# Two 256-column gating projections joined to one of 512 columns, and the spatial product moved behind the next projection's first steps

## The chip, the cores and the metric

The kernel runs on one core of a Trainium2 chip. The metric is the device time of one execution in microseconds; the time of a kernel is the median of its runs. Five engines work beside each other and wait for each other through semaphores: TensorE (PE) multiplies, VectorE (DVE) and ScalarE (ACT) work on tiles, GpSimd (POOL) does small pieces, and SyncE (SP) issues nearly all transfers. A matmul writes to PSUM, which has eight banks of 512 float32 columns; DVE or ACT must read a bank out before another result can take it.

## What is computed

One layer of a hybrid trunk for 1024 positions of 1024 channels. The part that matters here, cut from the reference:

```python
n = rms_norm(x, mix_norm_g[l])
proj = jnp.einsum('bsd,de->bse', n, w_in[l])
q, k, v, bg, cg, xh, su, sv = jnp.split(proj, cuts, axis=-1)
y_a = chunked_rel_attention(...)           # 8 heads of 64
y_b = gated_short_conv(bg, cg, xh, conv_w[l])
y_c = spatial_gating(su, sv, sg_ln_g[l], sg_ln_b[l], sg_w[l], sg_b[l])
...
# spatial_gating(u, v, ...), 256 channels each, blocks of 128 positions
u = jax.nn.gelu(u, approximate=False)
v = layer_norm(jax.nn.gelu(v, approximate=False), ln_g, ln_b)
mixed = jnp.einsum('gts,bnsgc->bntgc', tril(sg_w), vb) + sg_b
return u * mixed
```

Group norms, an output projection, a squared-ReLU MLP and a final norm follow; the change does not touch them.

## The kernel before

Every float32 product is made of three matmuls of a rounded high part and a remainder (`mm3`, lines 64 to 66): high by high, high by low, low by high. An operand is split by one ACT copy and one DVE subtraction (`split`, lines 52 and 53).

The front of the program runs in this order: the norm of x and the value projection; the key and query projections of head pair 0 (`qk_projs(0)`); `sgu`, the spatial gating; then the attention loop over 64 steps (four pairs, two heads, eight query tiles). Inside the loop the remaining projections run as fillers, in steps of three matmuls, and a table of knots (`target`) says how many filler steps are due at each attention step. The instructions of each engine are put in order by a scheduler that goes by program order and its own costs; each engine then works its list strictly in order.

In `sgu` the weights of the projection of v (`ws`, 256 columns) are split into slots that the attention uses later (`pth`, `ptl`). For each of eight tiles of 128 positions `token_proj` runs 24 matmuls of 256 columns into a PSUM tile `sv`; ACT applies GELU (`gv`, line 608), DVE and POOL do the layer norm (lines 610 to 616, `bs`, `mv`, `ms`, `rs`), and ACT and DVE split the result into `vh` and `vl`. Then a second loop does the same projection for u (`wu`, tile `su`, 24 matmuls of 256 columns for each tile, GELU at line 624). After it come the load of ACT's exponential table (line 625), `between()` (the expansion of the heads' operands, with the copies `v` at lines 300 and 301), and the spatial product: four groups `sg` of three matmuls of 512 columns, each read out by two DVE instructions (line 635, `u<-sg,cols,u`).

PSUM tiles are named by tags. `acc_tile` takes the tags of the list `ring` in turn. During `sgu` the list is `["acc", "S", "PT", "acc", "S"]`; after it, it is `["acc"]`, and a tag has two buffers. `s` are the scores of a step, `pr` its exponentials (line 485), `pt` their transposes, `pth` and `ptl` the split of these, `av` the product with the values. `kc` is both the raw weights of a key projection and, later, its result; `wh_k`, `wl_k`, `wh_q` and `wl_q` are split weights of pair 1 and take the slots (two for each tag) in which `wu` stood before.

Of the kernel before, what the change touches and what calls it, by code (L numbers as in the profile page):

```python
# [15 lines left out]
P = 128  # L16
# [4 lines left out]
HD = 64  # L21
# [9 lines left out]
def trunk(ctx, tc, x, mix_g, w_in, rb_rev, conv_w, sg_ln_g, sg_ln_b, sg_w, sg_b,  # L31
# [13 lines left out]
    def big(tag, shape, dt, name):  # L45
        return L.tile(shape, dt, tag=tag, bufs=SLOTS[tag], name=name)
# [16 lines left out]
    def mm3(ps, sh, sl, mh, ml, start, stop, **kw):  # L63
        PE.matmul(ps, lhsT=sh, rhs=mh, start=start, stop=False, **kw)  # L64
        PE.matmul(ps, lhsT=sh, rhs=ml, start=False, stop=False, **kw)  # L65
        PE.matmul(ps, lhsT=sl, rhs=mh, start=False, stop=stop, **kw)  # L66
# [69 lines left out]
    def acc_tile(name, tag=None):  # L136
        if tag is None:
            ring["i"] += 1
            tag = ring["tags"][ring["i"] % len(ring["tags"])]
        return psA.tile([P, 1024 if tag == "S" else HALF], F32, tag=tag, bufs=2,  # L140
                        name=name)[:, :HALF]
# [33 lines left out]
    def load_moving(c0, m, name, place):  # L175
        w = Moving(c0, m, name, place)
        for j in range(NK // w.kk):
            w.load(j)
            run(w.split(j))
        return w.ws  # L180

    def place_w(name):
        return lambda j, kk, m: (W.tile([P, kk, m], F32R, tag="wh", name=f"{name}h{j}"),
                                 W.tile([P, kk, m], F32R, tag="wl", name=f"{name}l{j}"))
# [6 lines left out]
    def token_proj(t, ws, m, name, between=None):  # L191
        hf, sl = t // 4, slice((t % 4) * P, (t % 4 + 1) * P)
        ps = acc_tile(name)[:, :m]
        for k in range(NK):
            if between and k == 4:
                between()
            mm3(ps, n.hi(hf, k)[:, sl], n.lo(hf, k)[:, sl], ws[k][0], ws[k][1],
                k == 0, k == NK - 1)
        return ps
# [247 lines left out]
    def scores(i):  # L447
        p, j, t, kb0, nfar = where(i)
        q2, kh, kl = heads[p, j]
        if t == 0:  # L450
            biases[p, j] = bias_tile(2 * p + j)
        if j == 0 and t == 0:
            ya[p] = big("VY", [P, T], F32, f"ya{p}")
        if j == 0 and t % 4 == 0:
            lsum[p, t // 4] = sm.tile([P, 8], F32, tag="lsum", bufs=4, name=f"lsum{p}{t // 4}")
        qs = q2[:, t * P:(t + 1) * P]
        s = prs[i] = wide(f"s{p}{j}{t}")

        near = slice((t - 1) * P, (t + 1) * P) if t > 3 else slice(0, max(2, t + 1) * P)
        end = HALF + near.stop - near.start  # L460
        if t > 3:
            ks = slice(kb0 * P, (t - 1) * P)
            PE.matmul(s[:, P:HALF], lhsT=qs, rhs=kh[:, ks], start=True, stop=False)
            PE.matmul(s[:, P:HALF], lhsT=qs, rhs=kl[:, ks], start=False, stop=True)
            V.memset(s[HD:P, P:P + HD], NEG)
        PE.matmul(s[:, HALF:end], lhsT=qs, rhs=kh[:, near], start=True, stop=False)
        PE.matmul(s[:, HALF:end], lhsT=qs, rhs=kl[:, near], start=False, stop=True)

    def softmax(i):
        p, j, t, kb0, nfar = where(i)  # L470
        s, bias = prs[i], biases[p, j]
        a = P if t > 3 else HALF
        b = a + (t - kb0 + 1) * P
        w = min(2, t + 1) * P
        st = sm.tile([P, 4], F32, tag="st", name=f"st{i}")
        V.tensor_tensor_reduce(out=s[:, b - w:b], in0=s[:, b - w:b], in1=bias[:, 256 - w:256],
                               op0=ALU.add, op1=ALU.max, scale=1.0, scalar=NEG, accum_out=st[:, 0:1])
        if nfar:
            V.tensor_reduce(st[:, 1:2], s[:, a:b - w], axis=AX.X, op=ALU.max)
            V.tensor_scalar(st[:, 2:3], st[:, 0:1], st[:, 1:2], -1.0, op0=ALU.max, op1=ALU.mult)  # L480
        else:
            V.tensor_scalar(st[:, 2:3], st[:, 0:1], -1.0, None, op0=ALU.mult)
        pr = AP_.tile([P, 640], F32, tag="P", bufs=3, name=f"pr{i}")
        lc = 2 * (t % 4) + j
        A.activation(pr[:, :b - a], s[:, a:b], AF.Exp, bias=st[:, 2:3],  # L485
                     accum_out=lsum[p, t // 4][:, lc:lc + 1])
        prs[i] = pr
# [95 lines left out]
    def sgu(u, between):  # L583
        sgw = raw_tile([P, 4, P], "sgw")
        load(sgw, sg_w.rearrange("g t s -> t g s"))
        ps = acc_tile("sgwT")
        for g in range(4):
            PE.transpose(ps[:, g * P:(g + 1) * P], sgw[:, g, :], ident)
        wsT = tmp("wsT").rearrange("p (g t) -> p g t", g=4)
        A.activation(wsT, ps.rearrange("p (g t) -> p g t", g=4), AF.Copy)  # L590
        G.affine_select(out=wsT, in_=wsT, pattern=[[0, 4], [1, P]], compare_op=ALU.is_ge,
                        fill=0.0, base=0, channel_multiplier=-1)
        wsh, wsl = [AP_.tile([P, 4, P], F32R, tag="P", bufs=3, name=f"wsT{a}") for a in "hl"]
        split(wsT, wsh, wsl)
        lnr = raw_tile([P, 2, 256], "lnr")
        load(lnr[:, 0, :], sg_ln_g.partition_broadcast(P))
        load(lnr[:, 1, :], sg_ln_b.partition_broadcast(P))
        ln = AP_.tile([P, 2, 256], F32, tag="P", bufs=3, name="ln")
        V.tensor_copy(ln, lnr)

        ws = load_moving(C_SU + 256, 256, "ws", lambda j, kk, m: [
            AP_.tile([P, 5, 256], F32R, tag=t_, bufs=2, name=f"ws{t_}{j}")[:, 0:kk] for t_ in ("pth", "ptl")])
        vh = [big("VY", [P, 2, NT, HD], F32R, f"vh{i}") for i in range(2)]
        vl = [big("VY", [P, 2, NT, HD], F32R, f"vl{i}") for i in range(2)]
        for t in range(NT):
            ps = token_proj(t, ws, 256, f"sv{t}")
            gv = tmp(f"gv{t}", m=256)
            A.activation(gv, ps, AF.Gelu)
            bs = sm.tile([P, 6], F32, tag="bs", name="bs")
            V.bn_stats(bs, gv)  # L610
            mv = sm.tile([P, 2], F32, tag="mv", name="mv")
            V.bn_aggr(mv, bs)
            r = rstd_of(mv[:, 1:2], 1, 1.0)
            V.tensor_scalar(gv, gv, mv[:, 0:1], r, op0=ALU.subtract, op1=ALU.mult)
            V.tensor_tensor(gv, gv, ln[:, 0], op=ALU.mult)
            V.tensor_tensor(gv, gv, ln[:, 1], op=ALU.add)
            g4 = gv.rearrange("p (i g e) -> p i g e", i=2, g=2)
            for i in range(2):
                split(g4[:, i], vh[i][:, :, t, :], vl[i][:, :, t, :])
        ws = load_moving(C_SU, 256, "wu", place_w("wu"))  # L620
        u += [big("VY", [P, 4, 256], F32, f"u{i}") for i in range(2)]
        for t in range(NT):
            ps = token_proj(t, ws, 256, f"su{t}")
            A.activation(u[t // 4][:, t % 4, :], ps, AF.Gelu)
        tc.keep_in_program_order(A.preload_act_table_set("exp_and_others"))
        between()
        for g in range(4):
            ps = acc_tile(f"sg{g}")
            i, j = g // 2, g % 2
            mm3(ps, wsh[:, g, :], wsl[:, g, :], vh[i][:, j].rearrange("p a b -> p (a b)"),  # L630
                vl[i][:, j].rearrange("p a b -> p (a b)"), True, True)
            for hf in range(2):
                us = u[hf][:, :, g * HD:(g + 1) * HD]
                pv = ps[:, hf * 256:(hf + 1) * 256].rearrange("p (a b) -> p a b", b=HD)
                V.scalar_tensor_tensor(us, pv, cols[:, 14 + g:15 + g], us, op0=ALU.add, op1=ALU.mult)

    def sgu_stat(u, rs):
        for hf in range(2):
# [33 lines left out]
            heads[0, j] = expand(0, j)  # L672
        expand_v(0)

    sgu(u, between)
    ring["tags"] = ["acc"]

    def gn_step(hfs=(0, 1)):
# [24 lines left out]
    def fill_to(x):  # L703
        while done["n"] < x:
            done["n"] += 1
            next(filler, None)

    def target(i):
        if i == 64:
            return 200  # L710
        p, k = i // 16, i % 16
        knots = ((0, 0), (12, 32), (16, 42)) if p == 0 else \
            ((0, 0), (2, 6), (12, 38), (16, 48)) if p < 3 else ((0, 0), (2, 6), (15, 55))
        base = (0, 42, 90, 138)[p]
        for (x0, y0), (x1, y1) in zip(knots, knots[1:]):
            if k < x1:
                return base + y0 + (y1 - y0) * (k - x0) / (x1 - x0)
        return base + knots[-1][1]

    scores(0)  # L720
    scores(1)
    softmax(0)
    for i in range(64):
        p, k = i // 16, i % 16
# [529 lines left out]
```

## Time and profile before

| | |
|---|---|
| median of 3 runs | 1130.63 us (1130.45 to 1135.13) |
| the profiled execution | 1133.42 us, its span 1131.7 us |
| PE busy | 97% of the span, 5377 matmuls |
| DVE, ACT, POOL busy | 66%, 49%, 6% |
| chain that ended last | PE 81%, DVE 8%, DMA 5% |

A line of the timeline begins with the start and the duration in us, then names engine, source line, operation and `out<-in` by tile names; brackets at its end give the time that the engine sat idle before it and what released it. Matmuls are pipelined: the start of one lies before the end of the one before, so the time that a run of matmuls takes is read from starts, not from durations.

### The profile page before, as it was taken

How to read it: one execution, taken by the hardware profiler on the slowest of the kernel's cores; microseconds unless marked ns; L12 is line 12 of the kernel's file. 1: busy time of each engine (PE TensorE's matmuls, PEld its weight loads, DVE VectorE, ACT ScalarE, POOL GpSimd, SP SyncE). 2: the span in 40 equal slices, each digit the busy share in tenths (PEclk: the TensorE clock that was granted, in tenths of full speed). 3: DMA queues.
4: the chain of work that ended last, by engine and by line, in shares of the span. 5: the costliest groups of instructions: out<-in, count | busy, mean ns of one | idle time of the engine just before them, and what ended most of it. 6: DMA issues, size and time to landing. Idle time of an engine off the chain costs nothing.

```text
span 1131.7 us, 14984 instructions
## 1 busy us (share of the span) xinstructions
PE 1094.5 (97%) x5377; PEld 913.2 (81%) x5377; DVE 748.5 (66%) x1430; ACT 549.6 (49%) x1094; POOL 73.0 (6%) x131
## 2 busy tenths in 40 slices
PE   7999999999999999999999999999959999999996
PEld 6879987887888788887888888888748888888885
DVE  5526487667676752579756565655597968879775
ACT  5434375655664520566555555555343434334452
POOL 1101023111011200000000000000000000000001
PEclk9999999999999899999999999999989999999998
DMA  7523013021120143453535353535787255253303
GB/s 248 173 63 85 1 24 98 8 69 33 39 61 19 58 148 112 168 205 121 204 113 192 115 186 121 179 119 185 280 324 269 96 176 175 86 201 107 103 19 148
DMA packets 82045, 145.16 MB, mean 128 GB/s; under 512 B 5922, under 2 KB 41524, under 8 KB 81972
## 3 DMA queue, kind: packets, MB, share of 16 engines
q1 hardware_dynamic: 81396, 142.38, 37.5%
q10 hardware_dynamic: 576, 1.84, 0.4%
q8 instruction: 42, 0.69, 0.3%
q14 instruction: 31, 0.25, 0.1%
HBM read 98.58 MB, written 41.42 MB: 124 GB/s over the span
## 4 chain that ended last, share of the span: by engine, by line
PE 81%; DVE 8%; DMA 5%; ACT 2%; issue 2%; POOL 1%; SPq 0%; POOLq 0%; DVEq 0%; ACTq 0%
PE dA L64 5%; PE dA L66 5%; PE dA L65 4%; PE uA L66 4%; PE uA L65 4%; PE uA L64 4%; PE dB L64 3%; PE dB L66 3%; PE dB L65 3%; PE av L537 3%; PE uC L64 2%; PE uC L65 2%; PE o L64 2%; PE uC L66 2%; PE o L65 2%; PE o L66 2%
## 5 line engine op out<-in xcount | busy, mean ns | idle before, releaser
L52 ACT ACTIVATE ho<-hr 128x512 fp32r<-128x512 f32 x112 | 68.7, 621 | 156.7 <-PE dA L66 68.4
L64 PE MATMUL dA<-wo,ho 128*128 128x512 f32 x256 | 100.5, 392 | 11.4 <-ACT ho L52 11.4
L66 PE MATMUL dA<-wo,ho 128*128 128x512 f32 x256 | 100.3, 392 | 0.0
L65 PE MATMUL dA<-wo,ho 128*128 128x512 f32 x256 | 100.3, 392 | 0.0
L53 DVE TENSOR_TENSOR ho<-hr,ho 128x512 fp32r<-128x512 f32 x112 | 76.2, 685 | 20.3 <-ACT ho L52 20.3
L64 PE MATMUL dB<-wo,ho 128*128 128x512 f32 x192 | 74.9, 390 | 0.2 <-ACT ho L52 0.2
L66 PE MATMUL dB<-wo,ho 128*128 128x512 f32 x192 | 74.9, 390 | 0.0
L65 PE MATMUL dB<-wo,ho 128*128 128x512 f32 x192 | 74.7, 389 | 0.0
L53 DVE TENSOR_TENSOR wo<-wd,wo 128x512 fp32r<-128x512 f32 x96 | 65.0, 684 | 2.4 <-ACT wo L52 2.4
L64 PEld LDWEIGHTS dA<-wo,ho 128*128 128x128 f32 x256 | 48.6, 190 | 21.8 <-ACT ho L52 11.8
L52 ACT ACTIVATE wo<-wd 128x512 fp32r<-128x512 f32 x96 | 58.3, 616 | 5.8 <-DVE wd L879 2.3
L485 ACT ACTIVATE pr<-s,st 128x640 f32<-128x640 f32 (+2 forms) x64 | 42.2, 660 | 36.9 <-DVE st L480 26.6
L876 DVE TENSOR_TENSOR acc<-dA,acc 128x512 f32<-128x512 f32 x64 | 44.0, 688 | 20.2 <-PE dA L66 18.2
L66 PEld LDWEIGHTS dA<-wo,ho 128*128 128x128 f32 x256 | 48.4, 189 | 10.8 <-DVE ho L53 0.6
L65 PEld LDWEIGHTS dA<-wo,ho 128*128 128x128 f32 x256 | 48.5, 189 | 10.0
L510 ACT ACTIVATE pth<-pt 128x512 fp32r<-128x512 f32 (+2 forms) x96 | 39.9, 434 | 32.1 <-PE pt L506 31.4
L511 DVE TENSOR_TENSOR ptl<-pt,pth 128x512 fp32r<-128x512 f32 (+2 forms) x96 | 45.2, 486 | 12.8 <-ACT pth L510 11.9
L64 PE MATMUL o<-woh,mxh 128*128 128x512 f32 x128 | 50.7, 399 | 0.0
L66 PE MATMUL o<-woh,mxl 128*128 128x512 f32 x128 | 50.5, 394 | 0.0
L65 PE MATMUL o<-wol,mxh 128*128 128x512 f32 x128 | 50.4, 394 | 0.0
L1175 POOL TENSOR_TENSOR rf<-ssf,mhalf 128x1 f32<-128x1 f32 x8 | 4.4, 549 | 629.9 <-DVE ssf L1173 629.9
L876 DVE TENSOR_TENSOR hid<-uC,v 128x512 f32<-128x512 f32 x15 | 10.4, 692 | 51.6 <-PE uC L66 51.6
(344 smaller groups left out, 3082.2 us busy)
## 6 DMA issues: line engine op xcount, KB each, us to landing
wr_u<-in_w_up SPq DMA_DIRECT2D x32, 512.0 KB, 4.5
wd<-in_w_down SPq DMA_DIRECT2D x32, 512.0 KB, 5.1
wr_o<-in_w_out SPq DMA_DIRECT2D x8, 512.0 KB, 4.4
xr<-in_x SPq DMA_DIRECT2D x8, 512.0 KB, 4.9
hs<-h SPq DMA_DIRECT2D x8, 512.0 KB, 3.7
acc<-hs SPq DMA_DIRECT2D x8, 512.0 KB, 9.3
out_y<-o SPq DMA_DIRECT2D x16, 256.0 KB, 2.1
x<-in_x SPq DMA_DIRECT2D x7, 512.0 KB, 4.0
```

Of the source, the lines that this page charges most:

```text
L52: A.activation(hi, raw, AF.Copy)
L53: V.tensor_tensor(lo, raw, hi.bitcast(F32), op=ALU.subtract)
L64: PE.matmul(ps, lhsT=sh, rhs=mh, start=start, stop=False, **kw)
L65: PE.matmul(ps, lhsT=sh, rhs=ml, start=False, stop=False, **kw)
L66: PE.matmul(ps, lhsT=sl, rhs=mh, start=False, stop=stop, **kw)
L485: A.activation(pr[:, :b - a], s[:, a:b], AF.Exp, bias=st[:, 2:3], accum_out=lsum[p, t // 4][:, lc:lc + 1])
L510: A.activation(dh, src, AF.Copy)
L511: V.tensor_tensor(dl, src, dh.bitcast(F32), op=ALU.subtract)
L537: PE.matmul(dst, lhsT=lhs, rhs=rhs, start=first, stop=(i == len(kbs) - 1 and ph == 1))
L876: V.tensor_tensor(out, a, b, op=ALU.add)
L1175: G.tensor_tensor(r, ss[:, 3:4], mhalf[:, 0:1], op=ALU.pow)
```

## The change

The two projections become one: the weights are the 512 columns from `C_SU` on, loaded in four blocks of two times 128 rows, two of them split into the attention's slots and two into the slots of `wu`. Each of eight `token_proj` calls now does 24 matmuls of 512 columns; ACT applies GELU to the two halves in two instructions. The spatial product is no longer issued inside `sgu`: `sgu` returns it as a function `mix`, which is called after the scores of the first two steps and after eight filler steps, and so after `ring` has become `["acc"]`. The knots of pair 0 begin at 8 instead of 0 and pass 34 instead of 32 at step 12.

```diff
-        ws = load_moving(C_SU + 256, 256, "ws", lambda j, kk, m: [
-            AP_.tile([P, 5, 256], F32R, tag=t_, bufs=2, name=f"ws{t_}{j}")[:, 0:kk] for t_ in ("pth", "ptl")])
+        ws = load_moving(C_SU, 512, "ws", lambda j, kk, m: place_w("ws")(j, kk, m) if j > 1 else [
+            AP_.tile([P, 1280], F32R, tag=t_, bufs=2, name=f"ws{t_}{j}")[:, 0:kk * m].rearrange(
+                "p (k m) -> p k m", k=kk) for t_ in ("pth", "ptl")])
...
+        u += [big("VY", [P, 4, 256], F32, f"u{i}") for i in range(2)]
         for t in range(NT):
-            ps = token_proj(t, ws, 256, f"sv{t}")
+            ps = token_proj(t, ws, 512, f"sv{t}")
             gv = tmp(f"gv{t}", m=256)
-            A.activation(gv, ps, AF.Gelu)
+            A.activation(gv, ps[:, 256:512], AF.Gelu)
+            A.activation(u[t // 4][:, t % 4, :], ps[:, 0:256], AF.Gelu)
...
-        ws = load_moving(C_SU, 256, "wu", place_w("wu"))
-        u += [big("VY", [P, 4, 256], F32, f"u{i}") for i in range(2)]
-        for t in range(NT):
-            ps = token_proj(t, ws, 256, f"su{t}")
-            A.activation(u[t // 4][:, t % 4, :], ps, AF.Gelu)
         tc.keep_in_program_order(A.preload_act_table_set("exp_and_others"))
         between()
-        for g in range(4):
-            ps = acc_tile(f"sg{g}")
...
+        def mix():
+            for g in range(4):
+                ps = acc_tile(f"sg{g}")
...
+        return mix
...
-    sgu(u, between)
+    mix = sgu(u, between)
     ring["tags"] = ["acc"]
...
-        knots = ((0, 0), (12, 32), (16, 42)) if p == 0 else \
+        knots = ((0, 8), (12, 34), (16, 42)) if p == 0 else \
...
     scores(0)
     scores(1)
+    fill_to(8)
+    mix()
     softmax(0)
```

PE's list at the spatial product. Before, the four groups stand in one piece right behind the last projection (the last two groups, the scores of step 0, and the key projection of pair 1):

```order
L64 MATMUL sg_1394<-vh_792,wsTh 128x512
L65 MATMUL sg_1394<-vl_794,wsTh 128x512
L66 MATMUL sg_1394<-vh_792,wsTl 128x512
L64 MATMUL sg_1400<-vh_792,wsTh 128x512
L65 MATMUL sg_1400<-vl_794,wsTh 128x512
L66 MATMUL sg_1400<-vh_792,wsTl 128x512
L466 MATMUL s_1411<-kh_1354,q_1356 128x256
L467 MATMUL s_1411<-kl_1355,q_1356 128x256
L64 MATMUL k_1445<-nh_138,wh_k_1441 128x512
```

Now the scores of steps 0 and 1 and 24 matmuls of the key projection come first; then the first group (`sg_1232`), the transpose of step 0 and the scores of step 2, and the rest as follows:

```order
L467 MATMUL s_1284<-kl_1155,q_1156 128x384
L64 MATMUL sg_1238<-vh_803,wsTh 128x512
L65 MATMUL sg_1238<-vl_805,wsTh 128x512
L66 MATMUL sg_1238<-vh_803,wsTl 128x512
L64 MATMUL sg_1244<-vh_804,wsTh 128x512
L65 MATMUL sg_1244<-vl_806,wsTh 128x512
L66 MATMUL sg_1244<-vh_804,wsTl 128x512
L506 MATMUL pt_1296<-ident,pr_1264 128x128 x2
L466 MATMUL s_1304<-kh_1154,q_1156 128x512
L467 MATMUL s_1304<-kl_1155,q_1156 128x512
L64 MATMUL sg_1250<-vh_804,wsTh 128x512
L65 MATMUL sg_1250<-vl_806,wsTh 128x512
```

The four groups moved behind 24 matmuls of `k`, and transposes and scores of the attention stand between them; the second half of the key projection follows the last group.

DVE's list at the read-out of the same groups in the changed kernel; the copies `v` (line 301) need ACT's copies of line 300, and `sg_1238` is the second group. The bias additions of a step print as ISA:

```order
L635 SCALAR_TENSOR_TENSOR u_807<-sg_1232,cols,u_807 128x4x64
L635 SCALAR_TENSOR_TENSOR u_808<-sg_1232,cols,u_808 128x4x64
L476 ISA s_1284,st_1290<-s_1284,bias_1182 128x256
L476 ISA st_1290 128x1
L635 SCALAR_TENSOR_TENSOR u_807<-sg_1238,cols,u_807 128x4x64
L301 TENSOR_TENSOR v_1172<-vf_227,v_1172 128x4x64 x2
L301 TENSOR_TENSOR v_1177<-vf_227,v_1177 128x4x64 x2
L635 SCALAR_TENSOR_TENSOR u_808<-sg_1238,cols,u_808 128x4x64
L635 SCALAR_TENSOR_TENSOR u_807<-sg_1244,cols,u_807 128x4x64
L635 SCALAR_TENSOR_TENSOR u_808<-sg_1244,cols,u_808 128x4x64
L635 SCALAR_TENSOR_TENSOR u_807<-sg_1250,cols,u_807 128x4x64
L635 SCALAR_TENSOR_TENSOR u_808<-sg_1250,cols,u_808 128x4x64
```

The four copies `v` stood between the two halves of the second group before the change too; what moved in front of this piece are the bias additions of steps 0 and 1, the split of `wl_q` and the layer norm of the last tile.

ACT's list from the split of the next key weights on, in the changed kernel (`gv_1135` and `sv_1110` belong to the last tile):

```order
L52 ACTIVATE wh_k_1197<-kc_1193 128x1024
L610 ACTIVATE gv_1135<-sv_1110 128x256
L611 ACTIVATE u_808<-sv_1110 128x256
L52 ACTIVATE wh_q_1217<-qc_1195 128x1024
L52 ACTIVATE vh_803<-gv_1135 128x2x64
L52 ACTIVATE vh_804<-gv_1135 128x2x64
L623 ACT_TABLE_LOAD
L485 ACTIVATE pr_1259,lsum_1186<-s_1187,st_1256 128x128
L388 ACTIVATE kc_1193<-k_1201 128x512
L485 ACTIVATE pr_1264,lsum_1186<-s_1190,st_1261 128x256
L510 ACTIVATE pth_1266<-pt_1272 128x128
L300 ACTIVATE v_1172<-vf_227 128x4x64 x2
```

Before, the table load followed the last GELU of `u` directly and the copies `v` came next; now the split of the last tile's layer norm stands ahead of the load, and the first exponentials behind it.

## Rows read from the trace of the kernel before

**Rows 1.** The page: busy times of PE to POOL, and the chain by engine.

```profile
PE 1094.5 (97%) x5377; PEld 913.2 (81%) x5377; DVE 748.5 (66%) x1430; ACT 549.6 (49%) x1094; POOL 73.0 (6%) x131
...
PE 81%; DVE 8%; DMA 5%; ACT 2%; issue 2%; POOL 1%; SPq 0%; POOLq 0%; DVEq 0%; ACTq 0%
```

**Rows 2.** Stretches: from:to length, PE, PEld, DVE, ACT, POOL busy (count), clock, DMA.

```profile
90.00:135.00 45.00, 45.00 (x378) 45.00 (x377) 24.51 (x70) 15.54 (x40) 6.33 (x15) 1.00 0.18 48
135.00:155.00 20.00, 20.00 (x108) 16.73 (x107) 16.02 (x50) 13.76 (x34) 0.00 (x0) 1.00 0.00 1
155.00:175.00 20.00, 20.00 (x122) 16.94 (x121) 16.65 (x51) 13.11 (x32) 10.44 (x11) 1.00 0.15 34
```

**Rows 3.** The tiles sv and su: count, shortest/median/longest ns, first and last start.

```profile
L64 PE MATMUL sv<-wspth,nh x64: 278/283/363, 89.6 to 112.3; 128*128 128x256 f32 x64
...
L66 PE MATMUL su<-wuh,nl x64: 283/283/283, 112.9 to 135.6; 128*128 128x256 f32 x64
```

**Rows 4.** PE's timeline, first and last of 18 matmuls in one run.

```profile
56.63 0.39 PE L64 MATMUL v<-wvh,nh 128*128 128x512 f32 x1
...
60.49 0.39 PE L66 MATMUL v<-wvh,nl 128*128 128x512 f32 x1
```

**Rows 5.** PE's timeline: first and last of the 12 products, two scores, the next matmul.

```profile
135.71 0.40 PE L64 MATMUL sg<-vh,wsTh 128*128 128x512 f32 x1
...
138.23 0.39 PE L66 MATMUL sg<-vh,wsTl 128*128 128x512 f32 x1
138.46 0.28 PE L466 MATMUL s<-kh,q 128*128 128x256 f32 x1
...
138.69 0.40 PE L64 MATMUL k<-nh,wh_k 128*128 128x512 f32 x1
```

**Rows 6.** Timelines of ACT and DVE around the end of the last projection.

```profile
134.47 1.06 ACT L52 ACTIVATE wh_k<-kc 128x1024 fp32r<-128x1024 f32 x1 [1.06 <-PE su L66]
...
135.56 1.22 DVE L53 TENSOR_TENSOR wl_k<-kc,wh_k 128x1024 fp32r<-128x1024 f32 x1 [12.53 <-ACT wh_k L52]
...
136.31 1.28 ACT L625 ACT_TABLE_LOAD   x1
137.61 1.34 ACT L300 ACTIVATE v<-vf 128x256 fp32r<-128x256 f32 x4
```

**Rows 7.** DVE's timeline: first and last step of one tile's layer norm.

```profile
116.11 0.43 DVE L610 BATCH_NORM_STATS2 bs<-gv 128x6 f32<-128x256 f32 x1
...
119.32 0.49 DVE L53 TENSOR_TENSOR vl<-gv,vh 128x128 fp32r<-128x128 f32 x2
```

**Rows 8.** ACT's timeline at the first attention steps.

```profile
142.95 0.37 ACT L485 ACTIVATE pr<-s,st 128x128 f32<-128x128 f32 x1 [3.06 <-DVE st L482]
143.22 0.19 ACT L485 ACTIVATION_READ_ACCUMULATOR pr<-s,st 128x1 f32 x1
...
145.85 0.60 ACT L388 ACTIVATE kc<-k 128x512 f32<-128x512 f32 x1 [0.61 <-PE k L66]
```

**Rows 9.** DVE's timeline at the read-out of the product.

```profile
138.06 1.43 DVE L301 TENSOR_TENSOR v<-vf,v 128x256 fp32r<-128x256 f32 x4
139.41 2.04 DVE L635 SCALAR_TENSOR_TENSOR u<-sg,cols,u 128x256 f32<-128x256 f32 x5
141.37 0.29 DVE L476 CUSTOM_DVE_ANT_0 s<-s,bias 128x128 f32<-128x128 f32 x1
...
141.58 1.22 DVE L53 TENSOR_TENSOR wl_q<-qc,wh_q 128x1024 fp32r<-128x1024 f32 x1
```

**Rows 10.** PE's timeline, the longest wait between 135 and 250 us.

```profile
196.28 0.33 PE L506 MATMUL pt<-ident,pr 128*128 128x128 f32 x1 [2.04 <-DVE ptl L511]
```

**Rows 11.** DMA issues (KB each, median us to landing), and PE's second wait before them.

```profile
wr_o<-in_w_out SPq DMA_DIRECT2D x8, 512.0 KB, 4.4
...
wr_ws<-in_w_in SPq DMA_DIRECT2D x2, 512.0 KB, 5.9
...
61.27 0.50 PE L64 MATMUL v<-wvh,nh 128*128 128x512 f32 x1 [0.39 <-ACT nh L119]
```

More of the change, by code (lines that the diff above doesn't have):

```diff
@@ L619, in sgu @@
                 split(g4[:, i], vh[i][:, :, t, :], vl[i][:, :, t, :])
-        ws = load_moving(C_SU, 256, "wu", place_w("wu"))
-        u += [big("VY", [P, 4, 256], F32, f"u{i}") for i in range(2)]
-        for t in range(NT):
-            ps = token_proj(t, ws, 256, f"su{t}")
-            A.activation(u[t // 4][:, t % 4, :], ps, AF.Gelu)
         tc.keep_in_program_order(A.preload_act_table_set("exp_and_others"))
         between()
-        for g in range(4):
-            ps = acc_tile(f"sg{g}")
[L629 to L635, printed above, removed]
+        def mix():
+            for g in range(4):
+                ps = acc_tile(f"sg{g}")
+                i, j = g // 2, g % 2
+                mm3(ps, wsh[:, g, :], wsl[:, g, :], vh[i][:, j].rearrange("p a b -> p (a b)"),
+                    vl[i][:, j].rearrange("p a b -> p (a b)"), True, True)
+                for hf in range(2):
+                    us = u[hf][:, :, g * HD:(g + 1) * HD]
+                    pv = ps[:, hf * 256:(hf + 1) * 256].rearrange("p (a b) -> p a b", b=HD)
+                    V.scalar_tensor_tensor(us, pv, cols[:, 14 + g:15 + g], us, op0=ALU.add, op1=ALU.mult)
+        return mix
     def sgu_stat(u, rs):
```

## The prediction

> **What bounds the kernel now.** I read the page first. PE is busy for 97% of the span and makes up 81% of the chain that ended last [rows 1], so a change in this part is worth what it does to PE: the time of its instructions, and its waits. Then the stretches around the change [rows 2]. From 90 to 135 us, the two projections, PE and its weight loads are busy without a break. From 135 to 155 us, the spatial product and the first attention steps, PE again does not stop, while DVE is busy for 16.0 of 20 us. The clock column is at 1.00 throughout, the 2.4 GHz level; nothing is to be had there. So before the change PE loses nothing here. The change can gain only by fewer or shorter PE instructions, and can lose by any wait that it makes.
>
> **The join.** It removes 384 matmuls of 256 columns and adds 192 of 512. The run of 384 begins at 89.6 us [rows 3] and the next instruction starts at 135.71 [rows 5]: 46.1 us, 0.120 us for each. A matmul of 512 columns in an unbroken run takes (60.49 - 56.63) / 17 = 0.227 us [rows 4]; the 12 of the spatial product took (138.46 - 135.71) / 12 = 0.229 [rows 5]. So 192 x 0.227 = 43.6 us, a gain of **2.5 us**; with 0.229 it is 2.1, and with the rounding of the starts at most 2.7. The second GELU of each tile (eight more in this run, eight fewer later) and the layer norms have 5.4 us a tile now, twice what they had, and ACT was busy for a third of this stretch [rows 2]: nothing.
>
> **The load in rows twice as long.** The four weight transfers keep their size, and their places between other transfers on SP's queue. `ws` took 5.9 us to land; transfers of the same size with the longer row, `wr_o`, took 4.4 [rows 11]. An earlier landing would shorten PE's wait of 0.39 us that comes from the ACT queue held up by the second `ws` block; but `ws` also landed among other transfers. I take 0, with 0.4 to either side.
>
> **The product moved.** I write T for the moment at which the last projection's matmuls have been issued (135.71 before). Before, 12 products followed at T with their operands long ready, each group in a bank of its own. Now PE does four score matmuls (0.23 us for two [rows 5], 0.47 in all), 24 of `k`, then the groups, and these have only the two `acc` buffers. I follow each wait.
>
> First, the split of the next key weights. `wh_k` takes the slot of the third weight block. ACT began it 1.24 us before T, when the first half of `wu` came free with twelve matmuls (1.44 us) to go [rows 6]; now it is free with six matmuls of 0.227 (1.36 us) to go, so ACT begins at T - 1.16 and DVE ends `wl_k` 1.09 + 1.22 us later [rows 6], at T + 1.15. Before, the products covered this. Now the third `k` matmul wants it at T + 0.93: a wait of **0.25** us (0 to 0.5).
>
> Second, the layer norm of the last tile. From `bs` to `vl` it took 119.32 + 0.49 - 116.11 = 3.7 us [rows 7]. DVE can start it after `wl_k`, and in between stand `wl_q` (1.22) and the bias additions of steps 0 and 1 (0.3 us for the first, the second with twice the columns) [rows 9], part of them in the gap that POOL leaves: `vh` is done at about T + 5.5 and `vl` at T + 5.9. PE needs them at 0.47 + 0.25 + 24 x 0.227 = T + 6.17. The 24 `k` matmuls hide it: **0**, and 0.5 if the covering 0.3 us is gone.
>
> Third, the exponential of step 0. On ACT's list the table load now stands behind the `vh` of the last tile. The load took 1.28 us [rows 6] and the exponential 0.37 [rows 8], so the transpose of step 0 can start at T + 7.3; PE has done the first group at T + 6.86. Wait **0.45** (0 to 1.0). In the rows the instruction behind the load started 1.30 us after it, so nothing beside the load itself was paid [rows 6]. The Trainium skill, "ScalarE: Activation LUTs", section "What ACT_TABLE_LOAD costs", adds a drain of some 1.38 us to every switch of sets. By the rows the wait is 0.45; by that rule it would be near 1.8 us.
>
> Fourth, the second group takes the bank of the first half of `k`, which ACT reads out (0.60) behind the exponential of step 0 and its accumulator read (0.19) [rows 8]: free at T + 8.0. PE, after the transpose and two scores of 0.44 us together, is there at T + 7.8. Wait **0.25** (0 to 0.5).
>
> Fifth, the fourth group takes the bank of the second one, and DVE reads that out in two pieces with the four copies `v` between them. The copies are paced by ACT (1.34 us for four [rows 6]), which reaches them only behind `kc`, the exponential of step 1 and a `pth`, at about T + 8.95. The last DVE copy ends near T + 10.65 and the second piece, 0.4 us each in a run of five [rows 9], at T + 11.1. PE, after groups two and three and step 3's scores, is there at T + 10.05. Wait **1.05** (0.3 to 1.6). Before, DVE had the same order and it cost nothing, because the four groups had four banks.
>
> Sixth, the second half of `k` takes the bank of the third group: two pieces more, T + 11.9, against PE's T + 11.8. Wait **0.1** (0 to 0.4).
>
> The waits sum to 2.1 us (0.3 at the lower ends, 4.5 at all upper ones, which is unlikely at once). The late read-outs push the scores' reductions on DVE back as well, but 15 matmuls of `k` (3.4 us) follow the last group before a transpose of step 2 is asked for, which I take as cover enough.
>
> **The rest.** The knots move two filler steps ahead of step 12 of pair 0; but eight steps are now due before the loop, so the density inside the loop stays. The longest wait further on, 2.04 us at 196 us [rows 10], hangs on the next key weights, whose load waits for the last heads of pair 0. In the two orders the same 21 filler matmuls lie between the last scores of pair 0 and the transpose that waits: 0.
>
> **The sum.** -2.5 + 2.1 = -0.4 us. The profiled execution took 1133.42 us and would take 1133.0. The median of the runs is 2.8 us lower, 1130.63, so I forecast **1130.2 us**: no change that can be told. About 0.5% of this kernel, 5.7 us, is what a measurement can tell from no change.
>
> **The rivals.**
>
> *The waits are covered.* If the read-outs keep ahead, only the join counts: -2.5 us, 1128.1. For it: PE does not stop from 135 to 175 us, though ACT and DVE do the same work there [rows 2]. Against it: the fifth wait comes from two banks and a fixed order on DVE, and no row gives it cover.
>
> *DVE falls behind, and it gets slower.* The place is the end of the first key projection. Eight read-outs of 0.41 us, 3.3 us in all [rows 9], now stand before the reductions of steps 2 and 3. Before, they were done 5.7 us after T (139.41 + 2.04); now they end some 13 us after T. If the exponentials of steps 2 and 3 are late by more than the 3.4 us of `k` matmuls that cover them, PE waits for most of those 3.3 us on top of the 2.1: -2.5 + 2.1 + 3.3 = +2.9, 1133.5. For it: DVE is busy for 16.65 of 20 us in the next stretch, too, and has little room to catch up [rows 2]. Against it: by my count the exponential of step 2 ends a microsecond before PE asks for it.
>
> *The switch of tables costs more than the load.* If the first exponential comes later by as much as the load again, PE waits 1.3 us more: -2.5 + 2.1 + 1.3 = +0.9, 1131.5. The row behind the load speaks against it [rows 6]. It is the drain of the skill's page named above, under "What ACT_TABLE_LOAD costs".
>
> *It does not do what it says*, in that the product is not hidden but only cut up: that is my forecast's own second half, so it has no chance of its own.
>
> **How the numbers follow.** My forecast has 0.65, covered waits 0.18, DVE behind 0.12, the costlier switch 0.05. The likeliest time is 1130.2. Its own bounds run from -2.7 - 0.4 + 0.3 (1127.8) to -2.1 + 4.5 + 0.4 (1133.4); the corners are unlikely, and I take 1128.0 to 1133.0. That takes in two of the rivals and leaves out the greater part of the DVE case. All cases lie within 5.7 us of the time before, so the chance of no measurable change is 0.93; 0.03 remains for faster by more than 0.5% and 0.04 for slower, for waits further on that no count here reaches.
>
> **What would show it.** In the profile of the changed kernel: 192 `sv` matmuls of 512 columns in 43.6 us; the table load behind the last `vh`; PE idle by 0.2 to 0.5 us before a `k` matmul, the first `pt` and the second `sg`, and by about 1 us before the last `sg`, released by DVE's line 635; then no wait until the 2 us one some 60 us later. It is wrong if PE runs through this stretch, if the transposes of steps 2 and 3 wait, or if the wait at 196 us changes by a microsecond or more.

## The result and the profile after

The changed kernel takes 1138.85 us, median of 9 runs (1135.9 to 1141.95), against 1132.2 of the kernel before in the same comparison: a ratio of 1.0056 with an interval of 1.0043 to 1.0069. It is slower by some 6 us where 0.4 us faster was forecast, and outside the range. The profiled execution took 1141.95 us, 8.5 more than that of before (1133.42).

The page of the changed kernel, busy times and the chain, against [rows 1]:

```profile
PE 1095.0 (96%) x5185; PEld 904.0 (79%) x5185; DVE 749.7 (66%) x1430; ACT 549.3 (48%) x1094; POOL 72.6 (6%) x131
...
PE 80%; DVE 9%; DMA 5%; ACT 3%; issue 2%; POOL 1%; SPq 0%; POOLq 0%; ACTq 0%; DVEq 0%
```

192 matmuls fewer, the same busy time, a longer span: PE's idle time grew by 8.0 us (37.2 to 45.2), and its busy time did not fall by the 2.5 us that the join takes off. Three stretches of the changed kernel, against [rows 2]:

```profile
90.00:135.00 45.00, 44.89 (x200) 36.89 (x200) 25.98 (x70) 16.46 (x39) 5.59 (x14) 1.00 0.18 47
135.00:155.00 20.00, 18.70 (x91) 14.74 (x89) 14.73 (x46) 11.65 (x29) 1.38 (x1) 1.00 0.00 1
155.00:175.00 20.00, 20.00 (x122) 16.86 (x121) 16.18 (x53) 13.37 (x35) 6.33 (x10) 1.00 0.14 34
```

PE, gapless from 90 to 175 us before, now stops for 1.3 us between 135 and 155. Waits of that size were forecast there, and they are far from 8.5. To find the rest I cut both programs at instructions that both have. PE's timeline of before at four cuts (first `sv`; first `xh`, a later filler projection; first `dA`, the start of the down projection; last product):

```profile
89.56 0.36 PE L64 MATMUL sv<-wspth,nh 128*128 128x256 f32 x1
...
240.19 0.48 PE L64 MATMUL xh<-nh,wh_xh 128*128 128x512 f32 x1
...
795.40 0.39 PE L64 MATMUL dA<-wo,ho 128*128 128x512 f32 x1
...
1120.52 0.39 PE L66 MATMUL dA<-wo,ho 128*128 128x512 f32 x1
```

The same four in the changed kernel:

```profile
89.27 0.48 PE L64 MATMUL sv<-wspth,nh 128*128 128x512 f32 x1
...
240.95 0.47 PE L64 MATMUL xh<-nh,wh_xh 128*128 128x512 f32 x1
...
798.50 0.39 PE L64 MATMUL dA<-wo,ho 128*128 128x512 f32 x1
...
1129.06 0.39 PE L66 MATMUL dA<-wo,ho 128*128 128x512 f32 x1
```

From `sv` to `xh`, the stretch that the change rewrites, the loss is 151.68 - 150.63 = 1.05 us. From `dA` to the end, the down projection, which the change does not touch, it is 330.56 - 325.12 = 5.4 us. Between these lie 2.3 us more.

**In the rewritten stretch.** PE's waits that stand out in the changed kernel:

```profile
140.38 0.33 PE L506 MATMUL pt<-ident,pr 128*128 128x128 f32 x1 [0.27 <-ACT pr L485]
...
144.22 0.47 PE L64 MATMUL sg<-vh,wsTh 128*128 128x512 f32 x1 [1.03 <-DVE u L635]
...
182.37 0.41 PE L537 MATMUL av<-pth,v 128*128 128x384 f32 x1 [1.51 <-DVE st L480]
...
198.65 0.33 PE L506 MATMUL pt<-ident,pr 128*128 128x128 f32 x1 [1.17 <-DVE ptl L511]
```

The bracket counts from the modelled end of the matmul before; the forecast counted from starts, and so counted the first two are 0.43 and 1.20 us. They are the third and fifth waits of the forecast; the last is the wait of [rows 10], shortened from 2.04. The one at 182 us is new. DVE and POOL just before it, in the changed kernel:

```profile
177.62 2.85 DVE L403 TENSOR_TENSOR q<-qc,q 64x1024 fp32r<-64x1024 f32 x1
...
177.48 1.91 POOL L653 TENSOR_TENSOR u<-u,rs 128x1024 f32<-128x1024 f32 x1
```

The same two in the kernel before:

```profile
179.39 1.22 DVE L403 TENSOR_TENSOR q<-qc,q 64x1024 fp32r<-64x1024 f32 x1
...
174.07 1.90 POOL L651 TENSOR_TENSOR u<-u,rs 128x1024 f32<-128x1024 f32 x1
```

Before, POOL's multiply of `u` ended 3.4 us ahead of the subtraction that expands the next head's `q`. Now POOL starts 0.14 us ahead of it, and the subtraction takes 2.85 us instead of 1.22, ending 1.08 us after POOL's end: as if it ran only then. A group of step reductions stands behind it on DVE, and PE's `av` waits for that.

**At the start of the down projection.** `hr` is a raw operand of the down projection as it is loaded; ACT and DVE split it into `ho`, which PE's products `dA` and `dB` read. SP's issues of the first two loads `hr` of the second step in the kernel before:

```profile
803.15 0.33 SPq L1139 DMA_DIRECT2D hr<-hd0a  x1
807.65 0.33 SPq L1139 DMA_DIRECT2D hr<-hd1a  x1
```

The same two in the changed kernel:

```profile
806.35 0.33 SPq L1143 DMA_DIRECT2D hr<-hd0a  x1
814.46 0.33 SPq L1143 DMA_DIRECT2D hr<-hd1a  x1
```

4.5 us apart before, 8.1 now, and PE's products `dB`, which need these loads, wait three times in the changed kernel (the longest such wait before was 0.16 us):

```profile
817.72 0.50 PE L64 MATMUL dB<-wo,ho 128*128 128x512 f32 x1 [1.34 <-ACT ho L52]
...
819.57 0.50 PE L64 MATMUL dB<-wo,ho 128*128 128x512 f32 x1 [0.63 <-ACT ho L52]
...
822.33 0.80 PE L64 MATMUL dB<-wo,ho 128*128 128x512 f32 x1 [1.43 <-ACT ho L52]
```

Behind the second of them the granted clock falls to the 1.2 GHz level for a while (stretches of the changed kernel; 1.00 in the corresponding two of before):

```profile
820.00:825.00 5.00, 3.57 (x9) 2.31 (x8) 2.52 (x5) 0.63 (x1) 0.00 (x0) 0.55 1.01 412
825.00:830.00 5.00, 5.00 (x18) 4.02 (x17) 2.60 (x5) 0.00 (x0) 0.00 (x0) 0.76 1.03 414
```

**Why there.** The addresses of the tiles in the two built programs show it. The pool `L` holds a ring `VY` of ten equal buffers; the builder hands a free buffer to whichever tile is written first. Before, `vh` and `vl` were written before `u0`; now the GELU of `u` stands in the same loop, ahead of the layer norm's result, so `u0` takes the buffer that `vh0` had and the others shift. The shift is passed on from owner to owner through the whole front. At its end `ho12`, an operand of the first down products, lies at bytes 62784 to 66879 instead of 66880 on. The tiles of the pool `down`, which takes the place of `L` for the down projection, have not moved: `hr<-hd1a` lands at 64832 to 66879. So its issue now waits until PE has read `ho12` for the last time, at the end of the first `dA` run, and SP's later loads stand behind it. SP's waits in the changed kernel from 790 to 822 us (total, times, longest), and ACT's split of this load:

```profile
SPq L1143 <- PE dA L66: 3.6, 1, 3.6
...
817.03 0.63 ACT L52 ACTIVATE ho<-hr 128x512 fp32r<-128x512 f32 x1 [1.94 <-DMA hr<-hd1a]
```

SP does not wait for `dA` at this place in the trace of before. That gives two theories. **Addresses**: the loss at 815 us comes from the ring's new order. **Arrival**: it comes from PE getting there a few us later, with its loads then meeting others.

### The profile page after: what moved, and what is told of

Read it like the earlier page. It is cut to its first block, busy times and chain, and to the rows that moved or that the text cites. A ratio compares the mean times of both kernels' runs of the same rounds, so it can differ in the third digit from the quotient of the medians.

```text
span 1140.2 us, 14599 instructions
## 1 busy us (share of the span) xinstructions
PE 1095.0 (96%) x5185; PEld 904.0 (79%) x5185; DVE 749.7 (66%) x1430; ACT 549.3 (48%) x1094; POOL 72.6 (6%) x131
## 4 chain that ended last, share of the span: by engine, by line
PE 80%; DVE 9%; DMA 5%; ACT 3%; issue 2%; POOL 1%; SPq 0%; POOLq 0%; ACTq 0%; DVEq 0%
PE dA L64 5%; PE dA L66 5%; PE dA L65 5%; PE uA L66 4%; PE uA L64 4%; PE uA L65 4%; PE dB L64 3%; PE dB L65 3%; PE dB L66 3%; PE av L537 3%; PE uC L64 2%; PE uC L65 2%; PE uC L66 2%; PE o L65 2%; PE o L66 2%; PE o L64 2%
## 5 line engine op out<-in xcount | busy, mean ns | idle before, releaser
L64 PE MATMUL dB<-wo,ho 128*128 128x512 f32 x192 | 76.2, 397 | 3.4 <-ACT ho L52 3.4
L66 PE MATMUL dB<-wo,ho 128*128 128x512 f32 x192 | 75.9, 396 | 0.0
L65 PE MATMUL dB<-wo,ho 128*128 128x512 f32 x192 | 75.7, 394 | 0.0
L511 DVE TENSOR_TENSOR ptl<-pt,pth 128x512 fp32r<-128x512 f32 (+2 forms) x96 | 45.2, 485 | 11.1 <-ACT pth L510 10.2
L64 PEld LDWEIGHTS dB<-wo,ho 128*128 128x128 f32 x192 | 36.7, 191 | 12.4 <-ACT ho L52 4.9
L880 DVE TENSOR_TENSOR acc<-dB,acc 128x512 f32<-128x512 f32 x48 | 32.9, 686 | 18.8 <-PE dB L66 18.8
```

What stands on the lines that cost most here:

```text
L511: V.tensor_tensor(dl, src, dh.bitcast(F32), op=ALU.subtract)
L880: V.tensor_tensor(out, a, b, op=ALU.add)
```

## The experiments

Times are medians, with the ratio to the kernel before, run on the same chip in the same comparison (1132.5 to 1132.8 us).

**1. The kernel before, with the ring in the new order.**

```diff
+        u += [big("VY", [P, 4, 256], F32, f"u{i}") for i in range(2)]
+        G.memset(u[0][:, 0, 0:1], 0.0)
         for t in range(NT):
             ps = token_proj(t, ws, 256, f"sv{t}")
```

(the later declaration of `u` is taken out).

> The kernel before, with u0 and u1 declared ahead of the first projection and one column of u0 set to zero on POOL there: PE, DVE, ACT and SP keep every instruction in its order, only the buffers of the ten-deep ring VY are dealt out differently, so that the operand ho12 of the first down products lies where the later load hr<-hd1a lands. Theory 'addresses': hr<-hd1a is issued some 7 to 8 us after hr<-hd0a instead of 4.5, PE dB waits on ACT ho come up three times (3 us in all) with a clock below 1.00 behind them, and the time is 4 to 6 us above the kernel before (the trace of the change stands at +3.2 before 812 us and at +8.6 after 839). Theory 'arrival' (the change's later lag and phase make the loads collide): within 0.7 us of the kernel before.

1136.87 us, ratio 1.0041 (1.0025 to 1.0056). SP's timeline in its trace:

```profile
797.52 0.33 SPq L1140 DMA_DIRECT2D hr<-hd0a  x1
806.15 0.33 SPq L1140 DMA_DIRECT2D hr<-hd1a  x1
```

PE's one wait at `dB`:

```profile
809.50 0.50 PE L64 MATMUL dB<-wo,ho 128*128 128x512 f32 x1 [1.44 <-ACT ho L52]
```

8.6 us apart, SP waiting 4.5 us for `dA`, with no other instruction of PE, DVE, ACT or SP moved. Addresses alone make the kernel slower. The profile fell on the fastest of the 12 executions (1129.88): there only one wait came, and the clock stayed up.

**2. The changed kernel, with `ho12` back in its old place.**

```diff
+        G.memset(vh[0].bitcast(F32)[:, 0, 0, 0:1], 0.0)
+        G.memset(vl[0].bitcast(F32)[:, 0, 0, 0:1], 0.0)
+        G.memset(vh[1].bitcast(F32)[:, 0, 0, 0:1], 0.0)
         for t in range(NT):
             ps = token_proj(t, ws, 512, f"sv{t}")
```

> The changed kernel, with one column each of vh0, vl0 and vh1 set to zero on POOL ahead of the projection, so that ho12 and wo12 lie where they lie in the kernel before; nothing else moves on PE, DVE, ACT and SP. Theory 'addresses': 4 to 6 us below the changed kernel, that is 1 to 3 us above the kernel before, with hr<-hd1a issued about 4.5 us after hr<-hd0a. Theory 'arrival': within 1 us of the changed kernel, 6 to 7 us above the kernel before.

1135.58 us, 1.0028 (1.0012 to 1.0045): 2.6 us under the changed kernel's 1138.21 of the same comparison, where 4 to 6 were expected, and 3.0 above the kernel before, the upper end of what was expected. Run 3, of 7 executions, has an interval that overlaps this one; the first comparison's for the changed kernel (1.0043 to 1.0069) does so only at its edge. The two issues, 4.2 us apart:

```profile
802.46 0.33 SPq L1146 DMA_DIRECT2D hr<-hd0a  x1
806.67 0.33 SPq L1146 DMA_DIRECT2D hr<-hd1a  x1
```

From `dA` to the end 325.62 us instead of 330.56. SP no longer waits for `dA`, and only one `dB` wait is left, 1.04 us. The traces overstate the gain: run 2's is of its fastest execution (1133.58), those of the changed kernel are of slow ones (1141.95, and 1140.64 in run 3). Of what remains above the kernel before, 1.4 us stand at `xh` and 1.1 from `uA` to `dA` in this trace (table below).

**3. The changed kernel again**, unchanged.

> The changed kernel once more. Both theories: 6 to 7 us above the kernel before. If its waits are properties of the program, av at 182 us waits about 1.5 us on DVE, and dB waits on ACT ho three times near 820 us again; if they are chance, they stand elsewhere or are gone.

1138.21 us, 1.0057 (1.0027 to 1.0086). Seven runs, from 1132 to 1143. `av` waits 1.5 us near 182 us again, `hr` is 8.4 us apart and `dB` waits twice (1.4 and 0.7 us) where three times were expected: the wait of `av` and the late `hr` are properties of the program, the number of `dB` waits is not.

**4. The join without the deferral**, with the three columns of run 2.

```diff
-    mix = sgu(u, between)
+    sgu(u, between)()
...
-    fill_to(8)
-    mix()
     softmax(0)
```

(and the old knots).

> The joined projection alone: the spatial product stands right behind it, as before the change, the steps' knots are the old ones, and the three columns are set to zero as in the second run, so the buffers at the start of the down projection are those of the kernel before. Theory 'addresses' with local costs as the trace of the change shows them: the join gives back 2.5 us, and PE waits for the last normalization from 132.9 to 138.6 us, 5.7 us, so 3 to 5 us above the kernel before (clock lost in the idle stretch included). Theory 'arrival' (any shift of a few us sets off the late losses): 7 us or more above.

1145.41 us, 1.0126 (1.0106 to 1.0146). PE's wait for the last tile's layer norm:

```profile
137.39 0.77 PE L64 MATMUL sg<-vh,wsTh 128*128 128x512 f32 x1 [5.17 <-issue]
```

The profile names no releaser; ACT's `vh` of that tile begins at 136.98 us. That part is as expected: 4.5 us lost at `xh`. The whole is not: 12.8 us above the kernel before is what *arrival* expected (7 or more). I had taken the ring for settled, and it was not. Here `t41h`, an operand of the very last product of the up projection, lies where the third of the early `wd` blocks lands, and the four loads were issued over 12.6 us, with SP waiting 11.1 us for PE's last `uA` products (4.8 before), instead of 6.4; `dA` to the end took 330.33 us. So a third order of the ring goes with the same loss of 5 us; no run put `t41h` back, so that it is the cause here is argued and not shown.

**5. POOL's multiplies of `u` later**, on run 2's kernel.

```diff
-        if p == 0 and k in (12, 14):
+        if p == 1 and k in (2, 4):
             next(norm)
...
-            G.tensor_tensor(u3, u3, rs[hf].unsqueeze(2).to_broadcast([P, 16, HD]), op=ALU.mult)
+            tc.keep_in_program_order(
+                G.tensor_tensor(u3, u3, rs[hf].unsqueeze(2).to_broadcast([P, 16, HD]), op=ALU.mult))
```

> The second run's kernel (changed kernel with ho12 where it lies in the kernel before) with the two multiplies of u on POOL (1.9 us each) kept behind the zeroing for pair 1's second probabilities; PE, DVE, ACT and SP keep their order. Theory 'POOL slows DVE': q<-qc at 177 us takes 1.22 us again instead of 2.85, the wait of av at 182 (1.5 us) goes, and the time is 0.7 to 1.6 us under the second run (part of it may come back in the wait for ptl at 198). Rival, that q is slow by itself at its place in the order: q still takes 2.8 us, time within 0.5 us of the second run.

DVE and POOL, with nothing else moved:

```profile
176.52 1.22 DVE L403 TENSOR_TENSOR q<-qc,q 64x1024 fp32r<-64x1024 f32 x1
...
198.98 3.77 POOL L657 TENSOR_TENSOR u<-u,rs 128x1024 f32<-128x1024 f32 x2
```

`q` is back at 1.22 us and the wait of `av` is gone; `sv` to `xh` takes 150.56 us instead of 152.03. The slow `q` was POOL's doing. The median, 1135.76 us, 1.0024 (1.0005 to 1.0043), does not show it: 12 runs from 1132 to 1141 do not resolve 1.5 us.

**6. The groups on two tags**, on run 2's kernel.

```diff
-                ps = acc_tile(f"sg{g}")
+                ps = acc_tile(f"sg{g}", ("acc", "PT")[g % 2])
```

> The second run's kernel with the four products sg0 to sg3 put by turns on the tags acc and PT, so that four banks stand ready instead of two. Theory of the prediction (fifth wait is for one of two banks): the wait of sg on DVE u (1.0 us) goes, 0.4 to 1.0 us under the second run; pt may wait instead for a PT bank (up to 0.5 us). Rival: DVE is short of time there, and the same microsecond shows as a wait of pt or av behind it: within 0.3 us of the second run.

1133.54 us, 1.0012 (0.9996 to 1.0028). That is 2.0 us under run 2, in another comparison, where 0.4 to 1.0 were expected. The only wait left among the twelve products is 0.16 us, for `kc`, and `xh` comes 1.9 us sooner. More than the banks changed: the scheduler now puts the four groups in one piece, ahead of the transpose of step 0, so the third wait is gone as well as the fifth (0.43 and 1.20 by starts). `q`, not touched here, still takes 2.83 us.

**7 and 10. Both edits**, twice.

> Both edits, on the second run's kernel. If the waits at the change's own place add up as PE's gaps show (1.0 and 1.5 us): 1.5 to 2.5 us under the second run, 0.5 to 1.5 us above the kernel before. If DVE or the loads behind set the pace: no more than 1 us under the second run.

> The seventh run's kernel once more (buffers, banks and POOL's multiplies mended). Its trace stood 1.4 to 1.8 us ahead of before at the first xh product, counted from the first sv product. If that gain reaches the end: 1 to 2 us under the kernel before. If it is lost in the stages behind, as the first comparison says: within 0.6 us of it.

1132.37 us, 1.0003 (0.9985 to 1.0021), and 1131.24 us, 0.999 (0.9977 to 1.0003). 3.2 and 4.3 us under run 2's median of another comparison, more than the 1.5 to 2.5 expected, and not to be told from the kernel before. `sv` to `xh` takes 148.80 and 148.70 us, 1.4 to 1.9 less than in the traces with the old front. Whether that reaches the end, run 10's question, the two medians answer differently (0.1 and 1.6 us under the kernel before).

**8. The deferral without the join**: two projections of 256 columns, the product behind eight filler steps. `ho12` falls on its old place by itself.

> The spatial product behind the first eight steps of the next projection, as in the change, but the two projections of 256 columns as in the kernel before; ho12 comes to lie as in the kernel before by itself. If the join is worth 2.5 us and the rest costs what the trace of the change shows (0.3, 1.0 and, where POOL still meets q, 1.5 us): 2.0 to 3.5 us above the kernel before or more, and dB at 812 us without the second and third wait. If the join were worth nothing, the second run's time would come out here, 3 us above the kernel before, with the same waits.

1134.91 us, 1.0019 (1.0005 to 1.0033). The projections themselves, from the first `sv` to the next matmul behind the run, take 46.15 us here and 43.66 with the join: 2.5 us. `sv` to `xh` takes 153.63 us, 1.6 more than with the join (run 2): the waits at the fourth group and at `av` are there (1.06 and 1.50 us), but the forecast's first and third, 0.7 us together, are not. The medians do not show the join: run 2 stands at 1.0028 and this run at 1.0019, so by time alone the join could as well be worth nothing.

**9. Run 1 again.**

> The first run's kernel once more, since its profile caught its fastest execution. Theory 'addresses': 3 to 5 us above the kernel before again; hr<-hd1a again 8 us behind hr<-hd0a; from the first dA product to the last product of the kernel 327 to 331 us, against 325.1 in the trace of before. If the first result was chance: within 1 us of the kernel before.

1134.93 us, 1.0023 (1.0009 to 1.0036): 2.1 us above the kernel before, less than the 3 to 5 expected, and slower all the same. `hr` is 8.2 us apart (802.07 and 810.23), `dB` waits 1.8 and 0.3 us, `dA` to the end takes 327.20.

**11 and 12. The loads of `acc4` to `acc7` and `gfin` later**, on the kernel before and on run 7's.

```diff
             load_down(BLOCKS[0], (0,))
+        if n == 1:
             for t in range(4, 8):
                 open_acc(t)
             load(gfin, fin_g.partition_broadcast(P))
```

> The kernel before, with the loads of acc4 to acc7 and gfin (2.5 MB) moved behind the loads hr<-hd0c to hd3c of the third down step. At 400 GB/s, the rate of the stretch from 815 to 835 us, they hold the queue 6 us; the wait of dA on ACT ho (11.4 us in the trace of before) should fall to 5 or 6 us, so 5 to 7 us under the kernel before. Rival, that everything loaded there is needed at once: the wait moves to the next steps, less than 2 us.

> The same move of the loads on the seventh run's kernel: the same gain again, 5 to 7 us under the kernel before, if the mended change is worth nothing in itself; 6 to 8 us if its gain of 1.4 to 1.8 us reaches the end.

1122.78 us, 0.9916 (0.9897 to 0.9934), and 1122.87 us, 0.9915 (0.9896 to 0.9934): both beat the kernel before by 10 us where 5 to 7 were expected. The long wait of `dA` for ACT's `ho`, 11.4 us in the trace of before, in run 11:

```profile
827.63 0.50 PE L64 MATMUL dA<-wo,ho 128*128 128x512 f32 x1 [2.25 <-ACT ho L52]
```

With the shorter pause the clock does not fall behind it (1.00 from 820 to 840 us, after 0.66 from 815 to 820 behind a wait at `dB`; 0.50 to 0.52 from 830 to 840 in the kernel before). The scheduler also put products and splits of the third and fourth steps in another order, so the 10 us are not the loads' alone. The mended change adds nothing that five runs of each can show.

The stretches of all traces side by side, each the difference of two starts on PE's timeline, in us (`o` is the first product of the output projection, `uA` the first of the up projection):

| trace | `sv` to `xh` | `xh` to `o` | `o` to `uA` | `uA` to `dA` | `dA` to end |
|---|---|---|---|---|---|
| before | 150.63 | 149.91 | 122.97 | 282.33 | 325.12 |
| 1, 9 (new ring) | 150.18, 150.64 | 149.62, 151.88 | 120.31, 120.30 | 282.41, 281.90 | 326.80, 327.20 |
| changed, 3 | 151.68, 151.91 | 151.95, 152.18 | 121.82, 120.47 | 283.78, 284.13 | 330.56, 330.58 |
| 2 (old place) | 152.03 | 150.50 | 120.35 | 283.47 | 325.62 |
| 5 (POOL later) | 150.56 | 152.65 | 122.47 | 283.17 | 325.88 |
| 6 (banks) | 150.15 | 152.00 | 120.26 | 282.81 | 326.07 |
| 7, 10 (both) | 148.80, 148.70 | 150.58, 150.00 | 120.35, 120.31 | 283.31, 282.96 | 325.62, 325.75 |
| 8 (no join) | 153.63 | 151.13 | 122.28 | 284.29 | 325.24 |
| 4 (no deferral) | 155.09 | 153.11 | 122.41 | 282.40 | 330.33 |
| 11, 12 (loads later) | 150.60, 148.87 | 149.94, 150.36 | 121.81, 121.85 | 282.08, 282.68 | 317.68, 316.67 |

The first column follows the edits, and the last one the places of the tiles and, in runs 11 and 12, the moved loads. The second and third move by 2 to 3 us in kernels of either front. In the second a key load lands earlier or later, and the clock falls behind it or does not. In the third PE waits nowhere; there the clock at its start differs (0.50 from 390 to 395 us in the trace of before, 1.00 in run 1's), behind the same three waits.

## Why the prediction was wrong

**The join**, -2.5 us: right. 192 matmuls in 132.92 - 89.27 = 43.65 us (43.6 forecast), and runs 2 and 8 differ by 2.5 us in the projections themselves, though not in their medians.

**The longer rows**: PE's wait in the value projection was 0.36 us, against 0.39 [rows 11]; nothing, as taken.

**The waits behind T**, 2.1 us in sum. First, `wl_k`: the third `k` matmul started 0.51 us behind the second (134.14 and 133.63) instead of 0.23, a wait of 0.28; 0.25 forecast. Second, the layer norm: hidden, as forecast. Third, 0.43 by starts for 0.45. Fourth, 0.25 forecast, and none came. Fifth, 1.20 by starts for 1.05; the trace names DVE's read-out as what ended it, and in run 6, with four banks and another order, it goes. Sixth, 0.1: none. Together 1.9 us, and the second half of `k` began at T + 12.1 (145.01 - 132.92) where T + 11.9 was forecast: the account of this stretch was right.

**The table load**: ACT's timeline in the changed kernel reads

```profile
138.57 1.28 ACT L623 ACT_TABLE_LOAD   x1
139.87 0.37 ACT L485 ACTIVATE pr<-s,st 128x128 f32<-128x128 f32 x1
```

1.30 us from start to start, the load and nothing more, as in [rows 6]. The rival with the costlier switch falls. The drain of the Trainium skill, "ScalarE: Activation LUTs", section "What ACT_TABLE_LOAD costs", is not seen in this case.

**The rest, taken as 0: this step failed, in two places.**

The first is in the front. The forecast counted who waits for whom through tiles and banks. It did not ask what POOL does while DVE works. The `rs` for the second half of `u` comes later now, so POOL's multiply meets DVE's subtraction, and that costs 1.5 us at `av` (run 5): a wait in the 60 us in which the forecast saw none, one of its own signs of being wrong. The wait at 196 us, said to stay, shrank by 0.9 (it was 1.58 us in run 1's trace, with the old front). Without that meeting the forecast's own sum nearly holds: run 5 stands at -0.1 to +0.4 us at `xh` against the traces with the old front (-0.4 forecast), and runs 7 and 10, without the third and fifth waits, at -1.4 to -1.9 (-0.4 - 0.45 - 1.05 = -1.9).

The second lies 680 us further on. The forecast read the order of the instructions and took memory as given: it did not ask whether a load would have to wait for a buffer. The new ring costs 2.6 us by the medians of runs 2 and 3, and 4.3 and 2.1 us by runs 1 and 9, where nothing else was moved: about 3 us. From `dA` to the end it is 5 us between the traces of the changed kernel and run 2's, and 1.7 and 2.1 in those of runs 1 and 9. SP's wait for `dA` is there in all four traces with the new ring (3.6 to 4.5 us), and is 0.2 us or none in the others. **Arrival alone falls**: run 1 came to the down projection 5 us earlier than before and still waited; run 5, counted from `sv`, came there within 0.4 us of the changed kernel and run 8 two us later, and both lost less than 1 us there. That a later arrival makes the new ring cost more is not excluded; no run took the two apart.

The medians lie 6.65 us apart, 7 from the forecast. Some 3 us for the ring, and 1.5 to 1.7 net in the front (1.05 and 1.28 lost at `xh` by the two traces of the changed kernel, -0.4 forecast), leave some 2.5. `uA` to `dA` is 0.3 to 2.4 us longer in every trace with the deferral. In the two traces of the changed kernel, 1.45 and 1.80 us longer than before, PE waits 1.49 and 1.87 us on DVE's `hid` (0.24 before), and ahead of that, near 550 us, ACT waits 2.84 and 3.22 us for a `wr_u` load (1.59 before). Why the load comes late, no run took apart: about a third of the miss stays open.

*DVE falls behind* had the right sign and the wrong mechanism: the transposes of steps 2 and 3 did not wait. Its count, read-outs ending some 13 us after T, was right (146.07 - 132.92 = 13.15), and the cover of 15 `k` matmuls was enough.

## What to carry to other kernels

In a program whose builder deals out buffers by order of first write, moving one tile's first write can change the addresses of everything that later shares its ring; where a later pool lies over that ring, a load may have to wait for an operand that is still being read. So compare the buffers and the waits of the built program around every change of pools, not only the order of instructions, and look at the loads that fill a new stage. When an instruction on POOL shifts, look at which DVE instructions with both inputs in SBUF it now runs beside.

## What the runs showed of the hardware

A DVE subtraction of 64x1024 from SBUF to SBUF took 1.22 us alone and 2.83 to 2.85 us when a POOL multiply of 1.91 us had begun just before it; moving the POOL instruction alone brought 1.22 back. The Trainium skill, "SBUF — State Buffer", section "SBUF: two separate sides", says that the port pair shared by the two is locked for a whole instruction, also against a DVE operation with two inputs in SBUF; the trace agrees, since the subtraction, which takes 1.22 us alone, ended 1.08 us after POOL did.

One and the same program varied by 10 us in 35 executions (the kernel before, 1128.4 to 1138.1). In traces of either front the load `kc` near 252 us made ACT wait for 1.4 to 2.7 us, and the clock sank to between 0.66 and 0.72 behind it in some and not in others. So two single profiles of this kernel can differ by several us without a cause in the program; this document compares them stretch by stretch.
